# Feed-forward of an encoder layer: split weights carried over a half switch, own places for the first block, and a residual added by transfers

## The chip, the cores and the metric

The kernel runs on one core of one Trainium2 chip. The metric is device time in microseconds (us) of one execution, given as the median of three. The engines are TensorE (PE, matrix products), VectorE (DVE), ScalarE (ACT), GpSimd (POOL) and SyncE (SP). SP computes nothing here: it issues nearly all transfers, one after the other.

## The reference

One layer of a trunk over 2048 tokens of width 1024, in float32. `att_*` weights serve windowed attention, `ffn_*` the feed-forward; `mod` comes from a conditioning vector.

```python
h = rmsnorm(x, mix_norm_pre[i]) * (1.0 + sc1) + sh1
y = windowed_gqa_sink(h, att_w_qkv[j], att_w_o[j], att_sink[j], rel_bias)
x = x + g1 * rmsnorm(y, mix_norm_post[i])          # called x1 in the kernel
h = rmsnorm(x, ffn_norm_pre[i]) * (1.0 + sc2) + sh2
a, b = split(h @ ffn_w_in[i]); y = (silu(a) * b) @ ffn_w_out[i]   # 2816 hidden units
x = x + g2 * rmsnorm(y, ffn_norm_post[i])          # the output
```

## The kernel before, in words

Activations stand transposed, 128 features by 512 tokens to a tile; 512 tokens are a chunk, c = 0 to 3, and two chunks are a half, hf = 0 and 1. The row is: projections, attention with the output projection (`OProj`) of chunks 0 to 2 as filler, the output projection of chunk 3 alone (`last_o`), the hidden stage, the out stage. A scheduler that simulates the program fixes the order on every engine and every buffer's address; at run time each engine takes its instructions in that order and waits at semaphores.

Products keep float32's accuracy by splitting each operand into a rounded part hi and a rest lo, and adding three products (`three`, L149 to L151). A split is one cast on ACT (L154) and one subtraction on another engine, mostly DVE (L155).

The feed-forward uses Strassen's scheme in Winograd's form. A half's two chunks and pairs of feature tiles make 2x2 blocks, and seven products replace eight. The seven operands from activations are called b11, t2, b21, t3, t1, t4, b22 (`OPERANDS`, in the order of the steps); tile names are such as `hb11…` and `ht2…`. The sums among them lie in DRAM: `hd_d` and `h2_d` for the hidden stage, `g_d` for the out stage. The seven from weights (`wa11, ws2, wa12, ws3, ws1, wa22, ws4`) are made on the spot by a `Block`: two loads (`wiri` or `wiro`, L741, L742), four sums on DVE (L746 to L749), seven splits. In a block `step(i)` runs product i over m tiles; `take` folds the product from PSUM into the results.

*Hidden stage.* Blocks t = 0 to 21 (`Hidden`) for each half. A half's operands stay in memory for all its blocks. At the switch from half 0 to half 1 the blocks 20 and 21 go step by step in turn (`interleaved`), and after each step that operand of half 1 is loaded. `give_pair` writes results to `g_d`. Beside half 0 runs the generator `late`: it turns chunks 2 and 3 of the attention's result into half 1's operands, one piece per block. Each chunk needs two statistics (`rstd_of`), whose sum over features is a product with a matrix of ones, after a split of the sum by DVE (L129, L130), as `nstl` and `nstlo`.

*Start of it.* `last_o` uses memory on the right side that the feed-forward gets afterwards (`lasto.close()`). The second pool for split weights, `wr`, and the pool `hB` for t1, t4 and b22 are opened only then. So the first block's last three split weights and those operands wait for the end of `last_o`.

*Out stage.* The 11 hidden tile pairs are cut into parts, `PARTS = ((2, 3, 3, 3), (3, 3, 3, 2))` by half. For each part four blocks `Outs` (n2 = 0 to 3) run; a part's last two blocks are interleaved while the next part's operands load. Part 0 copies its products to results z on ACT (L947), the others add them to z on DVE (L950). Half 0's end (`ends`) runs beside half 1's first parts: the statistic of z, then `finish` per tile, which is z times r (L998), then times a coefficient and plus x1 (L999) on DVE, x1 having been loaded by SP.

*Last part.* It is computed plainly: product `pl` for chunk 2 over 512 columns, then chunk 3 in two halves of 256. After the last product come the sum of squares (`nstz`, L126), the statistic, `finish` for eight tiles (L998, L999) and the stores.

Of the kernel before, what the change touches and what calls it, by code (L numbers as in the profile page):

```python
# [11 lines left out]
F32 = mybir.dt.float32  # L12
# [45 lines left out]
PARTS = ((2, 3, 3, 3), (3, 3, 3, 2))  # L58
MD = max(max(p) for p in PARTS)

# [13 lines left out]
def encoder_layer(ctx, tc, a):  # L74
# [43 lines left out]
    def rstd_of(alloc, psp, ptag, acc, tag, r=None, direct=False):  # L118
# [122 lines left out]
    with ExitStack() as pa:  # L241
# [9 lines left out]
        sp.dma_start(gains, a["gains"])  # L251
        act.activation(cb, cb, AF.Silu)
# [278 lines left out]
    class OProj:  # L531
# [5 lines left out]
        def fill(self, prev=None, hold=None):  # L537
# [11 lines left out]
            for n in range(KT):  # L549
                w = wop.tile([P, 2, KT, P], F32R, tag="w", name=f"wo{c}_{n}", bufs=2)  # L550
                if c in (0, NCH - 1):
                    raw = wop.tile([P, KT, P], F32, tag="raw", name=f"wor{c}_{n}", bufs=3 if c else 2)
# [21 lines left out]
                else:  # L574
                    sq = yp.tile([P, CH], F32, tag="nsq", name=f"ysq{c}_{n}", bufs=4)
# [110 lines left out]

    lasto = ExitStack()
# [11 lines left out]
    ffn = ExitStack()  # L699
# [3 lines left out]
    wl, wr = open_pool(early, "wl"), None  # L703
# [9 lines left out]
    class Operands:  # L713
# [6 lines left out]
        def slot(self, n, k):  # L720
            t = (hA if n in OPERANDS[:nleft] else hB).tile([P, 2, CH], F32R, tag=n, name=f"h{n}{self.u}_{k}")
            self.ops[n][k] = (t[:, 0], t[:, 1])
            return self.ops[n][k]
# [9 lines left out]
    class Block:  # L733
# [39 lines left out]
    def give_pair(hf, j):  # L773
# [5 lines left out]
        if hf == S // HALF - 1 and j >= HT // 2 - PARTS[-1][-1]:  # L779
# [5 lines left out]
    class Hidden(Block):  # L785
        def __init__(self, half, t, hf):
            super().__init__(half, t, f"i{half.u}_{t}", a["w_in"][t], a["w_in"][HT + t])
            self.t, self.got, self.hf = t, {}, hf
# [39 lines left out]
    def interleaved(pair, nxt, end=iter(())):  # L828

        for i in range(7):  # L830
            for b in pair:
                b.step(i)
            next(end, None)
# [3 lines left out]
    def late_residuals():  # L837

        for c in range(CPH, NCH):
# [13 lines left out]
            rstd_of(temp, psF, "mm", acc, f"l{c}", r)  # L853
            yield
            for k in range(0, KT, 2):
# [33 lines left out]
    wr = open_pool(ffn, "wr", side="right")  # L889
# [5 lines left out]
    for hf in range(S // HALF):  # L895
        for t in range(HT - 2 if hf + 1 < S // HALF else HT - 1):
# [3 lines left out]
            next(late, None)  # L900
        if hf + 1 < S // HALF:
# [3 lines left out]
            interleaved(pair, half)  # L905
    assert next(late, None) is None
# [250 lines left out]
```

## Time and profile before

| | |
|---|---|
| median of 3 runs | 2168.6 us (2166.22 to 2171.56) |
| profiled execution | 2170.63 us, span 2168.8 us, mean granted TensorE clock 0.98 |
| instructions | 28917 |
| busy: PE, DVE, ACT, POOL | 94%, 76%, 50%, 34% of the span |
| moved | 396.35 MB, mean 183 GB/s |
| hidden stage to out stage | about 1700 us |

Busy time of PE contains matmuls that overlap; how many matmuls a stretch holds says more of its rate. Where PE waits, the view of waits names the engine and line that ended the wait.

### The profile page before, as it was taken

How to read it: one execution, taken by the hardware profiler on the slowest of the kernel's cores; microseconds unless marked ns; L12 is line 12 of the kernel's file. 1: busy time of each engine (PE TensorE's matmuls, PEld its weight loads, DVE VectorE, ACT ScalarE, POOL GpSimd, SP SyncE). 2: the span in 40 equal slices, each digit the busy share in tenths (PEclk: the TensorE clock that was granted, in tenths of full speed). 3: DMA queues.
4: the chain of work that ended last, by engine and by line, in shares of the span. 5: the costliest groups of instructions: out<-in, count | busy, mean ns of one | idle time of the engine just before them, and what ended most of it. 6: DMA issues, size and time to landing. Idle time of an engine off the chain costs nothing.

```text
span 2168.8 us, 28917 instructions
## 1 busy us (share of the span) xinstructions
PE 2044.4 (94%) x9366; PEld 1669.0 (77%) x9366; DVE 1646.5 (76%) x2933; ACT 1076.9 (50%) x2125; POOL 747.7 (34%) x687
## 2 busy tenths in 40 slices
PE   6898999989989888999999989999999899998997
PEld 4786877878767766878887868888888688867886
DVE  7656766665676658987878898766664788999997
ACT  4546666577787746343434352333332654465432
POOL 3404343366778711533354512322221200230040
PEclk8999999999999989999999999999999999999998
DMA  8887665576667694534454764323230544447542
GB/s 279 261 256 250 187 184 172 165 275 244 226 196 241 199 342 174 192 130 155 170 169 156 257 232 148 123 96 117 102 112 35 194 151 150 147 147 271 167 139 102
DMA packets 200516, 396.35 MB, mean 183 GB/s; under 512 B 20091, under 2 KB 62124, under 8 KB 195244
## 3 DMA queue, kind: packets, MB, share of 16 engines
q1 hardware_dynamic: 199788, 393.97, 54.5%
q8 instruction: 74, 1.21, 0.2%
q14 instruction: 78, 0.64, 0.1%
q10 hardware_dynamic: 576, 0.52, 0.1%
HBM read 270.65 MB, written 123.76 MB: 182 GB/s over the span
## 4 chain that ended last, share of the span: by engine, by line
PE 66%; DVE 15%; DMA 7%; issue 4%; ACT 3%; POOL 3%; SPq 1%; DVEq 0%; ACTq 0%; POOLq 0%
PE pc_i L149 10%; PE pc_i L150 10%; PE pc_i L151 10%; PE pc_o L151 4%; PE pc_o L149 4%; PE pc_o L150 4%; PE t L455 3%; PE s L432 3%; PE psq L149 2%; PE psq L151 2%; PE psq L150 2%; PE py L149 2%; PE py L151 2%; PE py L150 2%; PE o L461 2%
## 5 line engine op out<-in xcount | busy, mean ns | idle before, releaser
L437 DVE CUSTOM_DVE_ANT_0 pr<-s,bias,nsink 128x384 f32<-128x384 f32 (+1 forms) x256 | 149.2, 596 | 93.7 <-PE s L432 73.2
L149 PE MATMUL pc_i<-ht,ws_i 128*128 128x512 f32 x528 | 207.1, 392 | 9.3 <-ACT ws_i L154 5.2
L151 PE MATMUL pc_i<-ht,ws_i 128*128 128x512 f32 x528 | 206.5, 391 | 0.0
L150 PE MATMUL pc_i<-ht,ws_i 128*128 128x512 f32 x528 | 206.4, 391 | 0.0
L439 ACT ACTIVATE pr<-pr,nm 128x385 f32<-128x385 f32 (+1 forms) x256 | 153.8, 603 | 70.5 <-DVE nm L437 63.2
L823 POOL TENSOR_TENSOR p_i<-p_i,u_i 128x512 f32<-128x512 f32 x44 | 72.1, 1638 | 323.5 <-DVE u_i L810 166.1
L445 POOL TENSOR_SCALAR pr<-pr,rs 128x384 f32<-128x384 f32 (+1 forms) x256 | 147.5, 601 | 82.4 <-DVE rs L443 82.3
L954 POOL TENSOR_TENSOR z<-z,z 128x512 f32<-128x512 f32 x32 | 54.8, 1730 | 344.3 <-DVE z L950 314.4
L432 PE MATMUL s<-k,q 128*128 128x384 f32 (+1 forms) x512 | 136.1, 359 | 19.8 <-DVE nm L437 13.5
L149 PE MATMUL pc_i<-hb,wa_i 128*128 128x512 f32 x352 | 138.5, 394 | 0.3
L150 PE MATMUL pc_i<-hb,wa_i 128*128 128x512 f32 x352 | 138.2, 393 | 0.0
L151 PE MATMUL pc_i<-hb,wa_i 128*128 128x512 f32 x352 | 138.2, 392 | 0.0
L154 ACT CAST ws_i<-s_i 128x512 fp32r<-128x512 f32 x132 | 81.7, 619 | 113.5 <-PE pc_i L151 100.6
L155 DVE TENSOR_TENSOR plo<-t,phi 128x512 fp32r<-128x512 f32 x184 | 121.6, 684 | 16.7 <-ACT phi L154 15.3
L154 ACT CAST wa_i<-wiri 128x512 fp32r<-128x512 f32 x132 | 81.8, 619 | 95.9 <-PE pc_i L151 93.7
L149 PEld LDWEIGHTS pc_i<-ht,ws_i 128*128 128x128 f32 x528 | 99.9, 189 | 32.1 <-ACT ws_i L154 5.7
L432 PEld LDWEIGHTS s<-k,q 128*128 128x128 f32 x512 | 86.6, 193 | 44.7 <-DVE nm L437 27.8
L455 PE MATMUL t<-ident,pr 128*128 128x128 f32 x736 | 113.1, 273 | 3.6 <-POOL pr L445 2.7
L150 PEld LDWEIGHTS pc_i<-ht,ws_i 128*128 128x128 f32 x528 | 99.9, 189 | 20.8
L151 PEld LDWEIGHTS pc_i<-ht,ws_i 128*128 128x128 f32 x528 | 99.7, 189 | 20.9
L149 PE MATMUL py<-ol,wo 128*128 128x512 f32 x256 | 103.3, 405 | 11.8 <-ACT wo L154 7.9
L155 DVE TENSOR_TENSOR wa_i<-wiri,wa_i 128x512 fp32r<-128x512 f32 x132 | 107.6, 816 | 5.4 <-ACT wa_i L154 5.1
(320 smaller groups left out, 6131.5 us busy)
## 6 DMA issues: line engine op xcount, KB each, us to landing
wiri<-w_in SPq DMA_DIRECT2D x88, 512.0 KB, 4.7
ada<-ada_w SPq DMA_DIRECT2D x40, 512.0 KB, 5.0
wiro<-w_out SPq DMA_DIRECT2D x48, 384.0 KB, 3.8
q_d<-e SPq DMA_DIRECT2D x64, 256.0 KB, 4.0
q<-q_d SPq DMA_DIRECT2D x16, 1024.0 KB, 5.8
wo<-wo_d SPq DMA_DIRECT2D x16, 1024.0 KB, 5.9
g_d_b<-p_i SPq DMA_DIRECT2D x44, 256.0 KB, 4.8
g_d_t<-p_i SPq DMA_DIRECT2D x40, 256.0 KB, 2.0
```

The costliest lines, as they stand in the source:

```text
L149: pe.matmul(ps, w[0], h[0], start=first, stop=False)
L150: pe.matmul(ps, w[0], h[1], start=False, stop=False)
L151: pe.matmul(ps, w[1], h[0], start=False, stop=last)
L154: act.copy(hi, src)
L155: return eng.tensor_tensor(lo, src, f(hi), ALU.subtract).ins
L432: m = pe.matmul(ps[:, :n], q[:, h, jb * P:(jb + 1) * P], kk[:, i, (jb + j0) * P:(jb + j1) * P], start=i == 0, stop=i == 1)
L437: red = dve.tensor_tensor_reduce(pr[:, h, :n], ps[:, :n], bias[g][:, h, j0 * P:j1 * P], -1.0, nsink[:, hh:hh + 1], ALU.add, ALU.min, nm[:, ...
L439: act.activation(pr[:, h, :n + 1], pr[:, h, :n + 1], AF.Exp, bias=nm[:, h:h + 1], scale=-1.0, accum_out=rs[:, h:h + 1])
L445: pool.tensor_scalar(pr[:, h, :n], pr[:, h, :n], rs[:, h:h + 1], 1.0, ALU.mult, ALU.mult)
L455: pe.transpose(pt[:, h * P:(h + 1) * P], pr[:, h, jj * P:(jj + 1) * P], ident)
L823: pool.tensor_tensor(sa, sa, b, ALU.mult)
L954: (pool if (i, x) in ((2, 2), (4, 4), (5, 5), (6, 6)) else dve).tensor_tensor(sums[hf, n2, x], sums[hf, n2, x], sums[hf, n2, y], ALU.add)
```

## The change

In the feed-forward and around it:

- **Half switch.** Half 1 begins with blocks 20 and 21 and takes over the split weights that half 0 has just used (`like`): no loads, no sums, no splits. Its other blocks are 0 to 19, and 19 is the last. In the out stage half 0's last part and half 1's first part are now the same tiles, 8 to 10, and half 1 begins with the pair n2 = 2, 3 on the weights that half 0 ended with. The plainly computed last part becomes tiles 6 and 7.
- **Places.** `wr` and a pool `hR` for operand t1 are opened before `last_o`'s pools, which shrink (two raw buffers in place of three, two of `nsq` in place of four in chunk 3). In the out stage there are 6 and 8 buffers of split weights (before 5 and 6), and two temporaries in place of five.
- **Late work.** `LATE` says how many pieces of `late` run after each block of half 0: none after the first three. The statistics there use the float32 sum directly, without DVE's split.
- **Statistics.** `rstd_of` has two DVE instructions in its end in place of three; the gains are multiplied by -0.5 once at the start, on POOL.
- **Residual.** `finish` is one DVE instruction; x1 is then added by a transfer that POOL issues and that accumulates into the tile, and SP's store waits for it. In `ends` the tiles have four buffers.
- **Last part.** Four quarters of 256 columns (half of a chunk); `ENDS` spreads earlier quarters' `finish` over later ones. The last quarter keeps a product and a sum with loaded x1 on DVE. The order of DVE's instructions there is fixed by tokens.

```diff
-PARTS = ((2, 3, 3, 3), (3, 3, 3, 2))
+PARTS = (((0, 2), (2, 3), (5, 3), (8, 3)), ((8, 3), (0, 3), (3, 3), (6, 2)))
+LATE = 3 * (0,) + 2 * (1, 1, 2, 1, 1, 1) + (1, 1, 2, 1, 1)
...
-        dve.scalar_tensor_tensor(t, ps, EPS, t, ALU.add, ALU.mult)
-        dve.tensor_scalar(t, t, -0.5, 1.5, ALU.mult, ALU.add)
-        dve.tensor_tensor(r, r, t, ALU.mult)
+        order(dve.scalar_tensor_tensor(t, ps, EPS, t, ALU.add, ALU.mult))
+        order(dve.scalar_tensor_tensor(r, t, -3.0, r, ALU.add, ALU.mult))
...
+    ffn = ExitStack()
+    wr = open_pool(ffn, "wr", side="right")
+    hR = open_pool(ffn, "hR", KT // 2, side="right")
     lasto = ExitStack()
...
-        def __init__(self, ops, i, u, wa, wb):
+        def __init__(self, ops, i, u, wa, wb, like=None):
             self.ops, self.u, m = ops, u, ops.m
+            if like is not None:
+                self.w = like.w
+                return
...
             sp.dma_start(acc, acc_d[c - CPH])
-            rstd_of(temp, psF, "mm", acc, f"lo{c}", r)
             yield
+            rstd_of(temp, psF, "mm", acc, f"lo{c}", r, direct=True)
...
     lasto.close()
-    wr = open_pool(ffn, "wr", side="right")
     hB = open_pool(ffn, "hB", K2, side="right")
...
-        for t in range(HT - 2 if hf + 1 < S // HALF else HT - 1):
+        for t in range(HT - 2 - hf):
...
-            next(late, None)
+            for _ in range(1 if hf else LATE[t]):
+                next(late, None)
...
             interleaved(pair, half)
+            interleaved([Hidden(half, b.t, hf + 1, b) for b in pair], None)
...
-    def finish(c, k, r, xr, cols=slice(0, CH), engs=(dve, dve)):
-        y, xr = ys[c, k][:, cols], xr[:, cols]
-        engs[0].tensor_tensor(y, y, r, ALU.mult)
-        engs[1].scalar_tensor_tensor(xr, y, coef[:, 3, k:k + 1], xr, ALU.mult, ALU.add)
-        (act if k % 2 and cols.stop - cols.start < CH and cols.start else sp).dma_start(out[c, :, k, cols], xr)
+    def finish(c, k, r, z, cols=slice(0, CH), order=lambda m: m):
+        z = z[:, cols]
+        order(dve.scalar_tensor_tensor(z, ys[c, k][:, cols], coef[:, 3, k:k + 1], r, ALU.mult, ALU.mult))
+        pool.dma_start(z, x1_d[c][:, k, cols], accum_op=ALU.add)
+        sp.dma_start(out[c, :, k, cols], z)
...
-            for n2 in range(KT // 2 - 2):
+            n2s = list(range(KT // 2))
+            if hf and p == 0:
+                n2s = n2s[2:] + n2s[:2]
+                like = [Outs(ops, hf, p, b.n2, b) for b in pair]
+                interleaved(like, None, end, 2)
...
+    parts = [(c, slice(i * CH // 2, (i + 1) * CH // 2)) for c in range(NCH - CPH, NCH) for i in range(2)]
...
+            if i and n == 3:
+                tail_rstd(i - 1)
+            for _ in range(ENDS[i][n] if n < KT else 0):
+                tail_finish(*ending.pop(0))
```

Line numbers shift by 4 to 40 in the new file; `three` is L153 to L155 there, a split L158 and L159.

**Order, first place: SP at the end of chunk 2's output projection.** `wo2_7` is that projection's last weight tile; `hd_d…` are stores of half 0's operands, `hf…` loads for them, `ol3…` the attention result that `last_o` multiplies. Before:

```order
L543 DMA ol3_0_8380<-o_d3_0_120 128x1024
L558 DMA wo2_7_8307<-wo_d7_351 128x2048
L469 DMA o_d3_3_123<-of15_3_8060 256x1x128
L611 DMA hd_d0_0_t3_305<-y1_0_6053 128x512
L579 DMA y_d0_340<-y2_5_8232 128x512
L502 DMA h2_d1_337<-y1_4_6625 128x512
L611 DMA hd_d0_0_t2_304<-y1_1_6244 128x512
```

Now:

```order
L616 DMA hd_d0_1_t1_310<-hf2_8237 128x512
L616 DMA hd_d0_0_t2_304<-y1_1_6240 128x512
L616 DMA hd_d0_0_t4_307<-hf1_8187 128x512
L614 DMA hf3_8238<-h2_d0_336 128x512
L507 DMA h2_d1_337<-y1_4_6620 128x512
L507 DMA h2_d1_337<-y1_5_6735 128x512
L563 DMA wo2_7_8300<-wo_d7_351 128x2048
```

The load of `wo2_7` stands behind a store of `t4` (from `hf1`, DVE's last sum of that group) and a load that it stood ahead of. The first `ol3` load, ahead of `wo2_7` before, comes here now:

```order
L616 DMA hd_d0_2_t4_315<-hf5_8289 128x512
L614 DMA hf6_8339<-h2_d0_336 128x512
L548 DMA ol3_0_8379<-o_d3_0_120 128x1024
L584 DMA y_d0_340<-y2_7_8327 128x512
L614 DMA hf7_8340<-h2_d0_336 128x512
L548 DMA ol3_1_8383<-o_d3_1_121 128x1024
L548 DMA ol3_2_8387<-o_d3_2_122 128x1024
```

Its wait there is for the last matmul of `py2_7`, whose memory it takes; the loads of `wor3_0` and `wor3_1` (`last_o`'s raw weights) have moved ahead of all these rows.

**Second place: ACT at the start of the hidden stage.** Casts of operands t4 (`ht40…`) and b22 (`hb220…`) and of split weights of block 0, 1 and 2 (`ws1_i0_0` is block 0's). Before:

```order
L154 CAST ht40_2_8796<-ht40_2_8796 128x512
L154 CAST ht40_3_8800<-ht40_3_8800 128x512
L154 CAST hb220_0_8804<-hb220_0_8804 128x512
L154 CAST hb220_1_8808<-hb220_1_8808 128x512
L819 ACT_TABLE_LOAD
L819 ACTIVATE p1_i0_0_8867<-p1_i0_0_8867 128x512
L154 CAST hb220_2_8812<-hb220_2_8812 128x512
L154 CAST hb220_3_8816<-hb220_3_8816 128x512
L154 CAST ws1_i0_0_8845<-s1_i0_0_8826 128x512
L154 CAST wa22_i0_0_8848<-wiri0_0_8823 128x512
L154 CAST ws4_i0_0_8851<-s4_i0_0_8828 128x512
L154 CAST wa11_i0_1_8988<-wiri0_1_8978 128x512
```

Now:

```order
L158 CAST wa11_i0_2_9116<-wiri0_2_9106 128x512
L158 CAST ws2_i0_2_9119<-s2_i0_2_9110 128x512
L158 CAST wa12_i0_2_9122<-wiri0_2_9106 128x512
L158 CAST ws3_i0_2_9125<-wiri0_2_9106 128x512
L158 CAST ht40_0_8784<-ht40_0_8784 128x512
L158 CAST ht40_1_8788<-ht40_1_8788 128x512
L158 CAST ws4_i0_1_8985<-s4_i0_1_8962 128x512
L158 CAST ws1_i0_2_9128<-s1_i0_2_9109 128x512
L158 CAST ht40_2_8792<-ht40_2_8792 128x512
L158 CAST ht40_3_8796<-ht40_3_8796 128x512
L158 CAST hb220_0_8800<-hb220_0_8800 128x512
L158 CAST hb220_1_8804<-hb220_1_8804 128x512
```

Block 0's weights are no longer in this stretch (they are split earlier); t4 and b22 have moved behind block 1's and much of block 2's weights. PE's order there, `pc5_i0_0` and `pc6_i0_0` being block 0's sixth and seventh product:

```order
L155 MATMUL pc4_i0_0_8910<-ht10_3_8780,ws1_i0_0_8841 128x512
L153 MATMUL pc5_i0_0_8926<-ht40_0_8784,wa22_i0_0_8844 128x512
L153 MATMUL pc6_i0_0_8941<-hb220_0_8800,ws4_i0_0_8847 128x512
L153 MATMUL pc0_i0_1_8988<-hb110_0_8695,wa11_i0_1_8967 128x512
L154 MATMUL pc0_i0_1_8988<-hb110_0_8695,wa11_i0_1_8967 128x512
```

PE takes one matmul each on the first t4 and b22 tile, and then goes on with block 1.

**Third place: DVE at the end of half 0's out stage**, where `z…` are half 0's results, `nrz0` their statistic and `zx…` what is stored. Before:

```order
L139 SCALAR_TENSOR_TENSOR ntz0_0_17899<-nstz0_0_17897,ntz0_0_17899 128x512
L155 TENSOR_TENSOR ws3_o1_0_3_18185<-wiro1_0_3_18166,ws3_o1_0_3_18185 128x384
L140 TENSOR_SCALAR ntz0_0_17899<-ntz0_0_17899 128x512
L141 TENSOR_TENSOR nrz0_0_17896<-nrz0_0_17896,ntz0_0_17899 128x512
L998 TENSOR_TENSOR z0_0_2_15779<-z0_0_2_15779,nrz0_0_17896 128x512
L998 TENSOR_TENSOR z0_0_5_15806<-z0_0_5_15806,nrz0_0_17896 128x512
L998 TENSOR_TENSOR z0_1_2_15873<-z0_1_2_15873,nrz0_0_17896 128x512
L998 TENSOR_TENSOR z0_1_5_15900<-z0_1_5_15900,nrz0_0_17896 128x512
```

Now:

```order
L144 SCALAR_TENSOR_TENSOR ntz0_0_17791<-nstz0_0_17789,ntz0_0_17791 128x512
L756 TENSOR_TENSOR s1_o1_0_1_18000<-wiro1_0_1_17997 128x384
L145 SCALAR_TENSOR_TENSOR nrz0_0_17788<-ntz0_0_17791,nrz0_0_17788 128x512
L757 TENSOR_TENSOR s2_o1_0_1_18001<-s1_o1_0_1_18000,wiro1_0_1_17997 128x384
L758 TENSOR_TENSOR wiro1_0_1_17997<-wiro1_0_1_17997 128x3x128
L159 TENSOR_TENSOR wa22_o1_0_0_17991<-wiro1_0_0_17966,wa22_o1_0_0_17991 128x384
L1003 SCALAR_TENSOR_TENSOR zx0_0_17797<-z0_0_2_15690,coef_361,nrz0_0_17788 128x512
L1003 SCALAR_TENSOR_TENSOR zx0_1_17801<-z0_0_5_15717,coef_361,nrz0_0_17788 128x512
L1003 SCALAR_TENSOR_TENSOR zx0_2_17829<-z0_1_2_15784,coef_361,nrz0_0_17788 128x512
L1003 SCALAR_TENSOR_TENSOR zx0_3_17833<-z0_1_5_15811,coef_361,nrz0_0_17788 128x512
```

The three instructions of a statistic are two, the product L998 is gone, and the finished tile is written by one instruction (L1003).

More of the change, by code (lines that the diff above doesn't have):

```diff
@@ L832, in interleaved @@
                 b.step(i)
-            next(end, None)
+            for _ in range(ends):
+                next(end, None)
             if nxt is not None:
@@ L1104, in _bucket @@
+    assert not ending
+    tail_rstd(3)
+    r = rs_[c][:, cols]
+    for n in range(KT + 1):
+        if n < KT:
+            y = ys[c, n][:, cols]
+            tail(dve.tensor_tensor(y, y, r, ALU.mult))
+        if n:
+            k, x = n - 1, late_x[n - 1]
+            tail(dve.scalar_tensor_tensor(x, ys[c, k][:, cols], coef[:, 3, k:k + 1], x, ALU.mult, ALU.add))
+            (act if k % 2 else sp).dma_start(out[c, :, k, cols], x)
 def _bucket(n):
```

127 lines of the change are left out of this document (66 added, 61 removed).

## The prediction

> **What bounds the kernel now.** I read the page's busy times and chain first, then stretches, then PE's waits, then the timeline where a wait is large.
>
> ```profile
> PE 2044.4 (94%) x9366; PEld 1669.0 (77%) x9366; DVE 1646.5 (76%) x2933; ACT 1076.9 (50%) x2125; POOL 747.7 (34%) x687
> PE 66%; DVE 15%; DMA 7%; issue 4%; ACT 3%; POOL 3%; SPq 1%; DVEq 0%; ACTq 0%; POOLq 0%
> ```
>
> PE is busy almost throughout, and the change takes no product away: it can only win back PE's pauses. The table of stretches shows where these are. The columns give PE's busy time, and in brackets how many matmuls began.
>
> ```profile
> core 0: us, PE busy (x) PEld busy (x) DVE busy (x) ACT busy (x) POOL busy (x), PEclk, DMA share, GB/s
> 740.00:780.00 40.00, 28.43 (x101) 21.36 (x100) 22.80 (x27) 19.31 (x26) 17.74 (x12) 0.83 0.94 341
> 820.00:860.00 40.00, 34.77 (x143) 28.16 (x142) 32.80 (x51) 22.78 (x37) 6.97 (x4) 0.91 0.54 191
> 900.00:960.00 60.00, 55.11 (x230) 44.71 (x229) 48.48 (x63) 22.32 (x38) 27.34 (x19) 0.94 0.47 156
> 1120.00:1160.00 40.00, 37.67 (x159) 30.72 (x158) 30.75 (x44) 17.41 (x28) 14.05 (x11) 0.96 0.44 145
> 1240.00:1320.00 80.00, 73.16 (x313) 57.79 (x312) 78.93 (x122) 35.37 (x65) 18.77 (x13) 1.00 0.66 227
> 1400.00:1480.00 80.00, 80.00 (x354) 66.24 (x353) 58.56 (x87) 25.73 (x43) 18.54 (x12) 1.00 0.30 105
> 1680.00:1720.00 40.00, 33.15 (x132) 25.56 (x131) 27.80 (x57) 23.62 (x50) 14.66 (x2) 0.94 0.57 204
> 1900.00:2000.00 100.00, 89.32 (x372) 69.60 (x371) 99.86 (x170) 61.94 (x122) 16.30 (x8) 0.97 0.60 207
> ```
>
> The row 1400 to 1480 has no pause: 354 in 80 us, 0.226 us each. Against that pace the others lack 76, 34, 35, 18, 41, 45 and 70 matmuls: 17, 8, 8, 4, 9, 10 and 16 us, 72 in all, slow clock after pauses included. Here are PE's waits from 740 us on, in us, with their number and the longest:
>
> ```profile
> PE pc_o L149 <- DVE z L950: 8.1, 3, 6.8
> PE py L149 <- ACT wo L154: 7.9, 1, 7.9
> PE nstl L131 <- DVE nhil L129: 6.0, 2, 3.7
> PE pc_i L149 <- ACT ws_i L154: 5.2, 1, 5.2
> PE py L149 <- DMA wo<-wo_d: 3.6, 2, 3.1
> PE pc_i L149 <- ACT p_i L794: 3.3, 2, 2.1
> ```
>
> **The change part by part.** The order before 740 us is shuffled by the shorter statistics; nothing there is aimed at, and I count 0, within 4 either way (a DVE instruction of 512 columns less per statistic, 0.68 us by the L528 row below).
>
> *End of chunk 2's projection.* Times of before, by queue and engine:
>
> ```profile
> 750.11 0.32 SPq L558 DMA_DIRECT2D wo<-wo_d  x1
> 756.09 0.68 DVE L528 TENSOR_TENSOR hf<-hf,y 128x512 f32<-128x512 f32 x1
> 763.34 1.71 SPq L543 DMA_DIRECT2D ol<-o_d  x2
> 765.61 0.69 ACT L570 ACTIVATE y<-py,coef 128x512 f32<-128x512 f32 x1 [7.89 <-PE py L151]
> 769.83 1.04 ACT L154 CAST ol<-ol 128x1024 fp32r<-128x1024 f32 x1 [3.04 <-DMA ol<-o_d]
> ```
>
> The load of `wo2_7` went out at 750.1 and PE waited 3.1 for it, to about 757.8. Now it stands behind the store of DVE's L528 (done at 756.8 before). DVE reaches that sum later: two splits of `last_o`'s weights stand ahead of it, and the statistic it hangs on ends later in PE's row. I put it at 757 to 758; four issues of about 0.4 follow, so the load goes out near 759.5, 9 us later, and PE's 3.1 grow to about 12. If DVE's splits don't wait, the load goes out as early as before, and nothing is lost; if they wait 2 us more, PE waits 14. Then `last_o`'s operand: its load could go out 2 us before the projection ended; now it must wait for that end. From issue (763.3) to the end of the first cast (770.9) took 7.5, so PE stands about 7.5 there again, instead of 7.9. The raw weights, which come earlier, no longer matter. Sum: +8 (range 0 to +11).
>
> *Start of the hidden stage.* The wait of 5.2 was for block 0's `ws1`:
>
> ```profile
> 821.58 0.69 ACT L570 ACTIVATE y<-py,coef 128x512 f32<-128x512 f32 x1 [3.10 <-PE py L151]
> 836.09 0.61 ACT L154 CAST ws_i<-s_i 128x512 fp32r<-128x512 f32 x1
> 836.61 0.61 ACT L154 CAST wa_i<-wiri 128x512 fp32r<-128x512 f32 x1
> ```
>
> It goes. But t4 and b22 are now cast behind nine casts of blocks 1 and 2, which themselves wait for the silu after block 0's third product. From the end E of `last_o` (821.5) PE has 32 matmuls, 7.2 us, before its first t4 matmul, and right behind it the first b22 matmul. ACT reaches the silu at E+3, block 1's sums on DVE hold its casts to about E+7.5, four of block 2 and then six (0.52 each by the last two rows) bring the first b22 cast to E+13. PE would wait about 5.5 in place of 5.2, with the same slow clock. I take -1 (range -7 to +2): the stall changes its name.
>
> *Late work.* The two waits for L129 (6.0) fall away with the split; a float32 sum costs PE about 0.45 us more than two rounded ones (the sums at the end, below: 3.6 us for eight of 256 columns, so 0.9 for 512, against 0.45), four times. The two waits for L794 (3.3) come when temporaries run short; the delay of three blocks meets them. I take -7 of the 12 that the stretches 900 and 1120 lack and these 3.3 (range -3 to -11).
>
> *Half switch.* DVE is busy 78.9 of 80 us, and it is what PE waits for. By form, in that stretch:
>
> ```profile
> L155 DVE TENSOR_TENSOR wa_i<-wiri,wa_i 128x512 fp32r<-128x512 f32 x12 | 11.3, 944 | 0.0
> L746 DVE TENSOR_TENSOR s_i<-wiri 128x512 f32<-128x512 f32 x4 | 3.8, 954 | 0.0
> ```
>
> Two blocks without four sums and seven splits each are 22 instructions of 0.68 to 0.95, 15 to 21 us off DVE, on the very stretch. Of the 9 us lacking I take -8 (range -4 to -9). The carried weights hold their buffers one pair longer; the next block's splits have that pair's 38 us (168 matmuls) to follow.
>
> *Hidden to out stage.* One POOL product took 13 us beside a row of DVE instructions, and SP's store of it held the loads behind it:
>
> ```profile
> 1698.66 13.34 POOL L823 TENSOR_TENSOR u_i<-u_i,b_i 128x512 f32<-128x512 f32 x1 [3.69 <-ACT u_i L819]
> 1712.03 0.33 SPq L778 DMA_DIRECT2D g_d_b<-u_i  x1
> ```
>
> The last block is now a pair whose sums go through DVE, so DVE itself waits for that product, and part 0's operand loads stand ahead of the store. Of 10 us I take -5 (range 0 to -8).
>
> *Out stage, 1900 to 2000.* DVE is busy 99.9 of 100 us; PE lacks 16.
>
> ```profile
> L998 DVE TENSOR_TENSOR z<-z,nrz 128x512 f32<-128x512 f32 x16 | 9.8, 681 | 0.1
> L155 DVE TENSOR_TENSOR ws_o<-s_o,ws_o 128x384 fp32r<-128x384 f32 x18 | 9.8, 544 | 0.0
> ```
>
> ```profile
> g_d_b<-p_i SPq DMA_DIRECT2D x44, 256.0 KB, 4.8
> ```
>
> L998's 16 products go (10 us), and two blocks' weights (22 instructions of about 0.55, 12 us): 22 us less on a saturated engine. I take -11 (range 0 to -15), since `finish` may now stop DVE: the fifth tile waits for the first one's accumulation and store. Neither an accumulating transfer nor one issued by POOL is in the trace; from the write (0.7) and two transfers like the page's `g_d_b<-p_i`, the nearest by size (4.8 each), a round takes about 10 us, against 13 DVE instructions of about 0.6 between. POOL's own combining (L954) then queues behind 16 issues, and frees z later; part 0 needs it only two pairs on.
>
> *End.*
>
> ```profile
> 2148.13 0.28 PE L150 MATMUL pl<-gls,wl 128*128 128x256 f32 x1
> 2148.25 0.28 PE L151 MATMUL pl<-gls,wl 128*128 128x256 f32 x1
> 2149.53 3.62 PE L126 MATMUL nstz<-zsl,ones 128*128 128x256 f32 x16
> 2155.96 0.47 ACT L136 ACTIVATE nrz<-nstz,epsc 128x256 f32<-128x256 f32 x1 [4.14 <-DVE z L998]
> 2155.78 3.25 DVE L999 SCALAR_TENSOR_TENSOR zx<-z,coef,zx 128x256 f32<-128x256 f32 x8
> 2160.18 2.77 DVE L998 TENSOR_TENSOR z<-z,nrz 128x256 f32<-128x256 f32 x8
> 2162.87 3.25 DVE L999 SCALAR_TENSOR_TENSOR zx<-z,coef,zx 128x256 f32<-128x256 f32 x8
> ```
>
> From the last product to the span's end pass 20.5 us. The sum of squares ends at 2153.2, but its logarithm starts at 2156.0 and DVE's part at 2159, behind the previous half's L999. With earlier quarters finished earlier: 4.9 to the end of the sums, 1.3 on ACT, 0.9 on DVE, 6.0 for L998 and L999, 2.7 from DVE's end to the span's: 15.8, so -4.7. Chunk 2 in halves costs 192 matmuls of 0.12 (the first two rows) for 96 of 0.226, +1.3. Sum -3.5 (range -6 to +4, if the 24 accumulations outlast the last quarter).
>
> Sum: 8 - 1 - 7 - 8 - 5 - 11 - 3.5 = -27.5. The profiled execution took 2170.6, 2.0 above the median; from the median the forecast is 2141.
>
> A rule speaks against the main doubt. By the Trainium skill, page "SBUF — State Buffer", section "Who interferes with whom", a DVE instruction with two inputs in SBUF holds up a GpSimd instruction that reads SBUF, not one that only writes. The POOL row of 13.34 us agrees with its first half; if the second holds, POOL's issues would not be starved, and the -11 stands; if they were, the rival below gives the time. No run of before shows an issue by POOL.
>
> **The rivals.**
>
> *The stalls only move.* The first two parts already do. If DVE stays saturated in the out stage because freed time is taken up by splits that the scheduler put earlier, -11 becomes -4, the half switch -4, hidden to out 0: about -12, 2157. For it: PE follows a fixed order. Against: 22 us off DVE.
>
> *Accumulation holds DVE* (slower). If each of POOL's issues is starved like the product of 13.3 us, a round of four tiles takes 13.3 and twice 4.8 and 0.7, 23.6 us; four rounds are 94 us beside a stretch whose products take 57 (252 matmuls). DVE stands at the fifth tile, PE behind DVE: +37 in place of -11, total about +20, 2189. It decides from a round of about 21 us. Against: DVE, once it waits, no longer starves POOL.
>
> *More than forecast.* The projection's end costs nothing (DVE gets there in time), and the ranges' better ends hold: about -50, 2119.
>
> *No change.* Gains of about 8 only, with the +8 of the first part and a longer end: 2167.
>
> **How the numbers follow.** Forecast 0.65, stalls move 0.16, more 0.09, accumulation 0.06, no change 0.04. The forecast's own range is 2125 to 2153. The range 2118 to 2160 takes in "more" and "stalls move", and leaves out the last two and some of the edges. A measurement of this kernel tells about 0.3%, 6.5 us, from no change: faster 0.87, same 0.06, slower 0.07.
>
> **What would show it.** Right: PE's wait for `wo<-wo_d` near 12 us; a wait for a cast of `hb` or `ht` in place of `ws_i` near 829; no `nhil` among the waits; 1240 to 1320 near 350 matmuls; 1900 to 2000 shifted, with over 415; under 17 us from the last `pl` to the end. Wrong: DVE waiting for stores at L1003, SP's loads late behind `out<-zx`, or a POOL product of over 10 us in the out stage.

## The result, and the profile after

The changed kernel takes 2191.6 us (median of 4 runs, 2187.8 to 2193.1) against 2170.1 us for the kernel before (4 runs, 2166.2 to 2173.6): ratio 1.0097, 95% interval 1.0074 to 1.012. It is slower by 1%, where 2141 was forecast. The profiled execution took 2193.05 us, its span 2191.1 us.

DVE lost the work that the change takes from it (1646.5 us before), and PE has 98 matmuls more, 96 of them from the chunk in halves:

```profile
PE 2055.1 (94%) x9464; PEld 1681.5 (77%) x9464; DVE 1594.1 (73%) x2857; ACT 1063.7 (49%) x2108; POOL 781.2 (36%) x728
```

So 52 us less on DVE bought nothing. The stretches after, with the columns as before (busy time and, in brackets, matmuls that began; full pace is 178 in 40 us, 531 in 120):

```profile
760.00:800.00 40.00, 18.17 (x58) 13.44 (x57) 24.33 (x22) 14.27 (x20) 13.52 (x8) 0.71 0.90 320
960.00:1000.00 40.00, 31.84 (x135) 25.89 (x134) 30.86 (x39) 15.01 (x25) 19.82 (x15) 0.91 0.59 191
1200.00:1240.00 40.00, 36.61 (x149) 29.38 (x148) 31.36 (x42) 17.48 (x26) 17.27 (x12) 0.91 0.61 207
1240.00:1360.00 120.00, 116.14 (x504) 93.77 (x503) 102.44 (x156) 44.63 (x78) 40.59 (x26) 1.00 0.65 226
1920.00:2040.00 120.00, 108.75 (x445) 85.61 (x444) 98.66 (x164) 61.18 (x120) 28.12 (x24) 0.96 0.63 178
```

The first row is the deepest hole: 58 matmuls, where before the poorest 40 us there had 101. PE's waits from 740 us on name its cause:

```profile
PE py L153 <- DMA wo<-wo_d: 14.5, 1, 14.5
PE pc_i L153 <- ACT p_i L804: 11.6, 2, 8.2
PE py L153 <- ACT ol L158: 7.2, 1, 7.2
PE pc_i L153 <- ACT ht L158: 3.0, 1, 3.0
PE pc_i L153 <- ACT hb L158: 2.6, 1, 2.6
PE py L153 <- ACT ysq L581: 2.1, 1, 2.1
```

Next I took the last matmul of each stage from the timeline, first of before, then of after: attention (`o`), output projection (`py`), hidden stage (`pc_i`), out stage (`pc_o`) and last part (`pl`, of before 2148.25).

```profile
747.21 0.39 PE L461 MATMUL o<-plo,v 128*128 128x512 f32 x1
821.15 0.40 PE L151 MATMUL py<-ol,wo 128*128 128x512 f32 x1
1692.87 0.40 PE L151 MATMUL pc_i<-hb,ws_i 128*128 128x512 f32 x1
2102.43 0.40 PE L151 MATMUL pc_o<-hb22o,ws_o 128*128 128x512 f32 x1
```

```profile
751.09 0.40 PE L466 MATMUL o<-plo,v 128*128 128x512 f32 x1
849.49 0.40 PE L155 MATMUL py<-ol,wo 128*128 128x512 f32 x1
1716.04 0.40 PE L155 MATMUL pc_i<-hb,ws_i 128*128 128x512 f32 x1
2125.79 0.40 PE L155 MATMUL pc_o<-hb22o,ws_o 128*128 128x512 f32 x1
2173.05 0.28 PE L155 MATMUL pl<-gls,wl 128*128 128x256 f32 x1
```

| stretch | before | after | difference | forecast |
|---|---|---|---|---|
| to attention's end | 747.2 | 751.1 | +3.9, with moved products +8.2 | 0 |
| output projection | 73.9 | 98.4 | +24.5, without moved products +14.7 | +8 |
| hidden stage | 871.7 | 866.6 | -5.2, with moved products 0 | start -1, late work -7, half switch -8 |
| out stage | 409.6 | 409.8 | +0.2 | hidden to out -5, out -11 |
| last part to its last `pl` | 45.8 | 47.3 | +1.4 | +1.3 |
| tail | 20.6 | 18.1 | -2.5 | -4.7 |

The moved products change the bookkeeping only. 24 matmuls of the first block (28 in place of 4) now stand ahead of the last `py`: at 0.226 us each 5.4 us. And 19 of chunk 2's projection now stand behind attention's last matmul (PE began 3425 matmuls up to there before, 3406 after): 4.3 us. The rows sum to 22.3 us, the difference of the spans.

The first row comes from one execution of each kernel and is not firm: all the kernels below that begin the same 3406 matmuls up to attention's end reach it between 744.8 and 752.0 us. The other rows repeat better; the projection takes 97.7 to 99.7 us in the seven kernels that have its long wait.

### The profile page after: what moved, and what is told of

Read it like the earlier page. It is cut to its first block, busy times and chain, and to the rows that moved or that the text cites. A ratio compares the mean times of both kernels' runs of the same rounds, so it can differ in the third digit from the quotient of the medians.

```text
span 2191.1 us, 29147 instructions
## 1 busy us (share of the span) xinstructions
PE 2055.1 (94%) x9464; PEld 1681.5 (77%) x9464; DVE 1594.1 (73%) x2857; ACT 1063.7 (49%) x2108; POOL 781.2 (36%) x728
## 5 line engine op out<-in xcount | busy, mean ns | idle before, releaser
L153 PE MATMUL pc_i<-ht,ws_i 128*128 128x512 f32 x528 | 206.0, 390 | 2.7 <-DVE p_i L809 0.8
L155 PE MATMUL pc_i<-ht,ws_i 128*128 128x512 f32 x528 | 205.7, 390 | 0.0
L159 DVE TENSOR_TENSOR plo<-t,phi 128x512 fp32r<-128x512 f32 x184 | 121.6, 685 | 26.2 <-ACT phi L158 24.9
L153 PE MATMUL pc_i<-hb,wa_i 128*128 128x512 f32 x352 | 139.9, 397 | 0.0
L155 PE MATMUL pc_i<-hb,wa_i 128*128 128x512 f32 x352 | 137.8, 391 | 0.0
L158 ACT CAST ws_i<-s_i 128x512 fp32r<-128x512 f32 x126 | 77.7, 618 | 121.5 <-PE pc_i L155 118.2
L158 ACT CAST wa_i<-wiri 128x512 fp32r<-128x512 f32 x126 | 78.1, 620 | 107.5 <-PE pc_i L155 107.2
L153 PE MATMUL py<-ol,wo 128*128 128x512 f32 x256 | 102.9, 406 | 25.3 <-DMA wo<-wo_d 14.5
L460 PE MATMUL t<-ident,pr 128*128 128x128 f32 x736 | 117.5, 279 | 4.4 <-POOL pr L450 3.6
L153 PEld LDWEIGHTS pc_i<-ht,ws_i 128*128 128x128 f32 x528 | 99.2, 188 | 24.9 <-issue 1.9
L154 PEld LDWEIGHTS pc_i<-ht,ws_i 128*128 128x128 f32 x528 | 99.3, 188 | 20.6
L155 PEld LDWEIGHTS pc_i<-ht,ws_i 128*128 128x128 f32 x528 | 99.1, 188 | 20.6
L158 ACT CAST phi<-t 128x512 fp32r<-128x512 f32 x184 | 101.5, 588 | 26.5 <-PE t L460 21.4
```

The lines of the kernel that those rows point to most:

```text
L153: pe.matmul(ps, w[0], h[0], start=first, stop=False)
L154: pe.matmul(ps, w[0], h[1], start=False, stop=False)
L155: pe.matmul(ps, w[1], h[0], start=False, stop=last)
L158: act.copy(hi, src)
L159: return eng.tensor_tensor(lo, src, f(hi), ALU.subtract).ins
L460: pe.transpose(pt[:, h * P:(h + 1) * P], pr[:, h, jj * P:(jj + 1) * P], ident)
```

## The experiments

Labels as c1 are those of the runs: c1 has places undone, c2 the load issued by ACT, c3 late even, c4, f3 and g1 the three on the kernel before, h1 the statistics of before, d1 and d2 the two pairs, d3 and f2 the carried weights, d4 and f4 the residual, f1 and h2 all three causes out. Each kernel below is the changed one with the edit shown, unless the text says "on the kernel before". The ratio is always to the kernel before, run on the same chip. "Late even" is one piece of late work after every block; "places" are the pools that the change opens ahead of `last_o`'s.

### Whose is the wait at the projection's end?

**Places undone.**

```diff
...
-    wr = open_pool(ffn, "wr", side="right")
-    hR = open_pool(ffn, "hR", KT // 2, side="right")
     lasto = ExitStack()
...
     lasto.close()
-    hB = open_pool(ffn, "hB", K2, side="right")
+    wr = open_pool(ffn, "wr", side="right")
+    hB = hR = open_pool(ffn, "hB", K2, side="right")
```

> The changed kernel with the places undone: the second pool of split weights and t1's operand are opened after the last output projection again, with its buffers as before (three raw, four of squares). Theory (the moved places set the order at the end of chunk 2's projection): the load of its last weight tile stands ahead of the t4 store again, PE's wait of 14.5 us for it falls under 4, the first operand of the last projection is loaded before that projection ends, and the total falls by 12 to 18 us, to 2174 to 2180; the wait for a cast of ht and hb at the start of the hidden stage (5.6) is replaced by one for ws_i of about 5. Rival (the shorter statistic alone sets that order): the 14.5 stays and the total moves by under 5.

Measured: 2168.1 us, ratio 0.9977 (0.9966 to 0.9987). The wait for `wo2_7` was 7.8, not under 4; the last `py` came at 824.65, and the total fell by more than the 12 to 18 us expected. One part of the change, undone, gives back all of the loss.

**Load of `wo2_7` issued by ACT**, past SP's queue.

```diff
-                    sp.dma_start(f(w), wo_d[n])
+                    (act if c == NCH - 2 and n == KT - 1 else sp).dma_start(f(w), wo_d[n])
```

> The changed kernel, but the load of chunk 2's last projection weight is issued by ACT and not by SP, so that it is behind nothing of SP's queue. Theory (the 14.5 us are SP standing before DVE's sums): the wait falls to 0 to 4 us, the total by 9 to 14, to 2178 to 2183; the wait for the last projection's first operand stays at about 7, since its load still has to wait for that projection's last matmul. Rival (the transfer itself is slow there, or DMA is full): the wait stays over 10.

Measured: 2177.3 us, ratio 1.0017 (1.0005 to 1.0029); wait 5.1, a little above the 0 to 4 expected. So the queue ahead of that load is the greater part of the wait, but the way round it doesn't reach what c1 does.

**On the kernel before: places alone, statistics alone, both.** The edits are the change's own.

```diff
-        dve.tensor_scalar(t, t, -0.5, 1.5, ALU.mult, ALU.add)
-        dve.tensor_tensor(r, r, t, ALU.mult)
+        dve.scalar_tensor_tensor(r, t, -3.0, r, ALU.add, ALU.mult)
...
```

> The kernel before with the places alone. Its order puts the last weight's load ahead of the t4 store, but the last projection's first operand behind it. Theory (both parts, places and shorter statistics, are needed for the 14.5): PE waits under 5 for the weight tile, about 7 to 8 for the operand, and at the start of the hidden stage about 5 for casts of ht and hb in place of ws_i: total within 5 us of before, 2165 to 2175. Rival (the places alone cost it): 10 to 20 us slower than before.

> The kernel before with the shorter statistics alone (two DVE instructions, gains scaled once). Its order moves the load of chunk 2's last projection weight behind ten more rows of SP, though not behind the t4 store. Theory (part of the 14.5 us comes from this part): PE's wait for that tile grows from 3 to 6 to 9 us, and the total by 2 to 8, to 2174 to 2181. Rival (the shorter statistics gain in attention what they lose there): within 2 us of before.

> The kernel before with both the places and the shorter statistics, nothing else. In its order the last weight's load stands behind the t4 store, as in the changed kernel and in neither of the two alone. Theory (the 14.5 us come from these two parts together): PE waits 12 to 15 us for that tile and 6 to 8 for the operand, and the total is 10 to 20 us above the 2166 of the shorter statistics alone. Rival (a third part, as the late work, is needed): the wait stays under 9.

Measured: places alone 2172.7 us, ratio 1.0006 (0.9992 to 1.002); statistics alone 2165.8, 0.9962 (0.9947 to 0.9977), where 2174 to 2181 was expected; both 2180.8, 1.0047 (1.0031 to 1.0063). PE's waits, one row of each in that order:

```profile
PE py L149 <- DMA wo<-wo_d: 3.4, 1, 3.4
```

```profile
PE py L148 <- DMA wo<-wo_d: 7.8, 1, 7.8
```

```profile
PE py L148 <- DMA wo<-wo_d: 15.3, 1, 15.3
```

Neither part makes the long wait (the statistics alone make half of it); together they do, and two parts that are neutral and faster alone come out slower. The mechanism is in the timeline. Statistic `nx` of chunk 2 (its second matmul on PE) and POOL's eight products with it, of before and then of after:

```profile
736.10 0.39 PE L132 MATMUL nstx<-nlox,ones 128*128 128x512 f32 x1
741.28 11.39 POOL L500 TENSOR_TENSOR y<-y,nx 128x512 f32<-128x512 f32 x8 [7.14 <-DVE nx L141]
```

```profile
749.46 0.39 PE L137 MATMUL nstx<-nlox,ones 128*128 128x512 f32 x1
755.54 13.76 POOL L505 TENSOR_TENSOR y<-y,nx 128x512 f32<-128x512 f32 x8 [0.63 <-DVE nx L145]
766.42 1.76 DVE L531 TENSOR_TENSOR y<-y,hf 128x512 f32<-128x512 f32 x1
768.21 1.64 DVE L533 TENSOR_TENSOR hf<-hf,y 128x512 f32<-128x512 f32 x1
769.87 0.32 SPq L616 DMA_DIRECT2D hd_d_t<-hf  x1
771.73 0.43 SPq L563 DMA_DIRECT2D wo<-wo_d  x1
```

With the shorter statistic that matmul stands 1.6 us ahead of attention's last one (751.09) where it stood 11.1 ahead (747.21), 13 us later in all; f3 and g1, which have the shorter statistic too, show the same place. POOL's products, DVE's sums and the t4 store follow 12 to 14 us later. The load of `wo2_7` goes behind that store only where both parts meet: issued at 771.7, not 759.5. With the statistics alone it goes out ahead of the sum (f3: 760.9, the sum at 770.5), and so it does with the places and the old statistics (h1 below: 751.9, the sum at 757.8). The same sums take 1.6 to 1.8 us here, beside POOL's products, against 0.68 before (the L528 row at 756.09, while POOL was idle).

**Statistics of before, rest as changed**, the test of that reading.

```diff
-        pool.tensor_scalar(gains, gains, -0.5, 1.0, ALU.mult, ALU.mult)
...
-        order(dve.scalar_tensor_tensor(r, t, -3.0, r, ALU.add, ALU.mult))
+        order(dve.tensor_scalar(t, t, -0.5, 1.5, ALU.mult, ALU.add))
+        order(dve.tensor_tensor(r, r, t, ALU.mult))
```

> The changed kernel with the statistics of before (three DVE instructions, gains not scaled); all else as changed. Theory: the two-instruction statistic moved chunk 2's statistic nx about 13 us later in every engine's order (its second matmul 736.1 before, 749.5 after), with it POOL's eight products and DVE's sums, and the places put the load of wo2_7 behind the last of these. With the old statistic nx comes early again: its last instruction about 6 us ahead of the end of attention instead of 3 us behind it, POOL's products of L505 before about 755, PE's wait for wo<-wo_d 3 to 5 us in place of 14.5, a wait for ol of 8 to 10, last py 12 to 16 us earlier against the end of attention, time 2175 to 2180. Rival: the places alone make the wait (smaller buffers for wor and nsq): the wait stays at 12 to 15 and the time at 2188 to 2193.

```profile
PE pc_i L154 <- ACT p_i L804: 13.3, 1, 13.3
PE py L154 <- ACT ol L159: 10.1, 1, 10.1
PE py L154 <- DMA wo<-wo_d: 4.0, 2, 3.5
```

```profile
742.96 11.40 POOL L505 TENSOR_TENSOR y<-y,nx 128x512 f32<-128x512 f32 x8 [7.16 <-DVE nx L146]
```

The mechanism came out as expected: POOL's products at 743, the wait 4.0, the load issued at 751.9, and the last `py` 83.6 us behind attention's end against 98.4. The time followed only in part: 2186.2 us (2182.3 to 2189.2), ratio 1.0066 (1.0048 to 1.0085), above the 2175 to 2180 expected. In the profiled execution, the fastest of the four, the projection's 14.8 us are there, but the hidden stage was 3.7 us longer and the out stage 2.3. The late work's stall at 980 us grew (first row) and a later one went: from 900 to 1240 us PE began 1416 matmuls, against 1422.

### Late work

**Late even.**

```diff
-LATE = 3 * (0,) + 2 * (1, 1, 2, 1, 1, 1) + (1, 1, 2, 1, 1)
+LATE = 20 * (1,)
```

> The changed kernel with one piece of the late work after each block of half 0 (as before the change), the statistics still on the float32 sum. Theory (thicker late work makes ACT's copies wait): PE's waits for the cast or copy of p_i, 11.6 us in two places, fall to under 5, the total by 6 to 12, to 2180 to 2186. Rival (they come from other changes, as the order of loads): they stay, within 3 us.

Measured: 2180.2 us, ratio 1.0036 (1.0024 to 1.0047). The hidden stage took 859.5 us in place of 866.6, and the stretch 960 to 1000 has no pause left:

```profile
960.00:1000.00 40.00, 40.00 (x177) 32.73 (x175) 30.75 (x44) 16.45 (x27) 12.55 (x8) 1.00 0.35 119
```

The stall that it removes, on ACT and DVE of the changed kernel:

```profile
990.07 0.69 DVE L513 TENSOR_TENSOR ly<-ly,lx 128x512 f32<-128x512 f32 x1 [2.63 <-POOL ly L512]
990.85 0.63 ACT L519 ACTIVATE xsq<-ly 128x512 f32<-128x512 f32 x1 [4.34 <-issue]
991.38 0.57 ACT L804 COPY p_i<-pc_i 128x512 f32<-128x512 f32 x1
```

ACT's copy of a product, for which PE waits 8.2 us, stands in ACT's order behind a square of the late work, which waits for a chain SP, POOL (L512), DVE (L513). My reading is that two pieces after one block bring more such squares than the chain can feed in that time; that even pieces remove the stall is shown. They also undo the delay of three blocks; with 20 pieces for 20 blocks no run has the delay without the density.

**Places undone and late even; the same with the load by ACT.**

> The changed kernel with places undone and the late work even, both at once. Theory (the two losses are independent): what the two runs alone won adds up, 23 and 11 us, so 2155 to 2161, faster than the kernel before by 11 to 17 us. Rival (once one wait is gone the other grows): no better than 2165.

> The same, and the load of chunk 2's last projection weight issued by ACT. With places undone PE still waited 7.8 us for that tile; by ACT it should wait 2 to 5: total 3 to 6 us under the kernel with both undone. Rival (the wait is the transfer beside the other loads): no difference over 2 us.

Measured: 2162.4 us, ratio 0.9947 (0.993 to 0.9963), and 2164.3, 0.9957 (0.9943 to 0.997). The two causes nearly add: 29 us where the two alone gave 23 and 11, just above the 2155 to 2161 expected. The load by ACT cut the wait from 7.8 to 4.4 and the projection by 1.9 us (72.5 to 70.5), but the total shows no gain.

### The carried weights

**Half 1's first pair splits its weights again**, in the hidden stage (d3), in the out stage (f2).

```diff
-            interleaved([Hidden(half, b.t, hf + 1, b) for b in pair], None)
+            interleaved([Hidden(half, b.t, hf + 1) for b in pair], None)
```

```diff
-                like = [Outs(ops, hf, p, b.n2, b) for b in pair]
+                like = [Outs(ops, hf, p, b.n2) for b in pair]
```

> The changed kernel, but half 1's first two hidden blocks load, sum and split their weights again, in the same order of blocks. Theory (DVE's saved work is what shortens the half switch): PE lacks 6 to 12 us more between 1240 and 1400 than in the changed kernel (27 matmuls, 6 us there), total +4 to +10. Rival (the order of blocks, in turn by pairs, gives the time, not the saved work): within 2 us.

> The changed kernel, but half 1's first pair of out blocks loads, sums and splits its weights again. Theory (the saved 12 us of DVE are of use): PE lacks 3 to 12 us more between 1920 and 2040, total 2194 to 2204. Rival (DVE isn't the limit there any more; SP's order is): within 3 us of the changed kernel.

Measured: 2191.2 us, ratio 1.0077 (1.0061 to 1.0094), and 2196.9, 1.0106 (1.0084 to 1.0129). Neither can be told from the changed kernel by its time. The stretches say a little more: 1240 to 1360 of d3, then 1920 to 2040 of f2.

```profile
1240.00:1360.00 120.00, 114.63 (x496) 91.97 (x495) 110.84 (x169) 49.48 (x88) 37.51 (x25) 1.00 0.66 232
```

```profile
1920.00:2040.00 120.00, 103.54 (x414) 80.39 (x414) 102.98 (x174) 62.54 (x127) 30.35 (x24) 0.93 0.64 189
```

Without the carry 8 matmuls fewer at the half switch (2 us) and 31 fewer in the out stage (7 us). The stages agree: d3's hidden stage is 2.7 us longer than that of the changed kernel, f2's out stage 7.1.

### The residual by transfers

**Half 0's finish on DVE** with x1 loaded by SP, as before.

```diff
-                finish(c, k, r, z)
+                sp.dma_start(z, x1_d[c][:, k, :])
+                dve.tensor_tensor(ys[c, k], ys[c, k], r, ALU.mult)
+                dve.scalar_tensor_tensor(z, ys[c, k], coef[:, 3, k:k + 1], z, ALU.mult, ALU.add)
+                sp.dma_start(out[c, :, k, :], z)
```

> The changed kernel, but in half 0's end x1 is loaded by SP and product and sum stand on DVE as before; the tail is left. Theory A (the accumulating transfers hold SP's queue, 33 us of waits, and so the next part's operands): PE lacks less between 1920 and 2040 than the 19 us of the changed kernel, by 5 or more. Theory B (DVE's saved 11 us outweigh that): it lacks 5 to 11 us more. Neither: within 3, the transfers trade one wait for another.

**Half 0's stores issued by POOL**, the accumulation kept.

```diff
-        sp.dma_start(out[c, :, k, cols], z)
+        (sp if c >= NCH - CPH else pool).dma_start(out[c, :, k, cols], z)
```

> The changed kernel, but in half 0's end POOL issues the store behind each accumulating transfer, so that SP's queue waits for none of them. Theory (SP standing before those stores is what delays the next part's operands): the out stage wins most of the 10 us that finishing on DVE won, total 2180 to 2186. Rival (DVE's wait for one of four buffers is what costs): DVE waits the same or more, no gain, 2189 or more.

Measured: 2181.1 us, ratio 1.0032 (1.0018 to 1.0046), and 2186.3, 1.0053 (1.0039 to 1.0068), the second just above its 2180 to 2186. The stretch 1920 to 2040 of the two (x445 in the changed kernel):

```profile
1920.00:2040.00 120.00, 115.24 (x491) 93.43 (x491) 113.04 (x190) 66.09 (x128) 13.94 (x8) 0.97 0.58 193
```

```profile
1920.00:2040.00 120.00, 112.88 (x469) 90.03 (x468) 101.94 (x171) 63.71 (x126) 37.31 (x40) 0.96 0.63 184
```

With 14 us more work on DVE the stretch holds 46 matmuls more, and the out stage takes 399.6 us in place of 409.8. In the changed kernel two in-order rows wait there, DVE's and then SP's:

```profile
DVE zx L1003 <- DMA out<-zx: 11.5, 7, 2.3
```

```profile
SPq L1005 <- DMA zx<-x_d: 32.7, 15, 6.2
```

SP's stores wait 32.7 us for POOL's accumulations, and what stands behind them on SP is the loads of the next operands. DVE's seven waits are for one of four buffers. Moving the stores off SP gave 24 of the 46 matmuls back, with DVE's waits unchanged (11.0): about half of the cost is SP's queue (by the length of the out stage 3.9 of the 10.2 us). In that run the stores wait in POOL's queue instead, 24.0 us, so the other half is not shown to be DVE's waits.

### All three causes out

**Places undone, late even, half 0's finish on DVE; and the same with the places kept and the statistics of before.** No new edit.

> The changed kernel with places undone, late work even, and half 0's end finished on DVE with loaded x1: all three losses found so far taken away, the carried weights, the direct statistics and the tail kept. Theory (they add): 11 us below the 2162 of the kernel with the first two undone, if nothing else fills the gap: 2149 to 2157, faster than before by 15 to 22 us. Rival: in that kernel the out stage had already lost less, so the gain there is under 4, 2158 or more.

> The changed kernel with the statistics of before, one piece of late work after each block, and half 0's finish as product and sum on DVE with x1 loaded by SP; places and carried weights stay. Theory: the three causes add (about 13, 11 and 10 us of 2191.6): 2155 to 2160, and no better than with the places undone (2154), since the operand wait of 8 to 10 us at the end of the projection stays in place of a wait of 4 us for block 0's weights. Rival: with the wait for wo2_7 gone, the places pay after all (last_o begins earlier and block 0's weights are ready): 2143 to 2150.

Measured: 2154.1 us, ratio 0.9909 (0.9894 to 0.9925), and 2158.3, 0.9935 (0.991 to 0.9961). Both beat both kernels. What is left of the change in the first (mainly carried weights, shorter statistics, the last part in quarters) makes the kernel 0.9% faster. No run shows that the places pay: without the long wait h2, which has them, is not faster than f1, which has not (the intervals overlap, and the statistics differ too), and on the kernel before they were neutral (c4). At the projection's end and behind it PE waits 9.7 us for `ol`, 4.0 for `wo<-wo_d` and 2.6 for `hb` in h2, and 7.9 for `wo2_7` and 4.4 for `ws_i` in f1.

## Why the prediction was wrong

Forecast -27.5, measured +22 in the profiled runs. By the rows of the table, moved products put back, the projection cost 14.7 us in place of 8, the hidden stage gained nothing in place of 16, the out stage with its start nothing in place of 16, and attention's end came 8.2 later in place of 0, which is not firm. Most of the miss is thus gains that did not come. Two steps failed above all: that a delay of the late work frees PE, where its denser rest stalls ACT; and that the accumulation costs DVE a wait and SP nothing. Three further gains were too large, and one cost was too small.

*End of chunk 2's projection, +8 forecast, +14.7 measured: wrong in size.* The queue position was right (the load stands behind the t4 store), and so was the operand wait (7.5 forecast, 7.2 measured). The failing step is "I put it at 757 to 758" for DVE's last sum; it came at 768.2. The prediction saw that the statistic ends later in PE's row, but gave it a microsecond or two where it took 13, since the shuffle before 740 us was counted at 0. That this late statistic makes the wait is shown by h1, where it is early and the wait 4.0, and that it needs the places beside it by f3 and g1. The wait itself, 14.5 where about 12 was forecast, came near by luck: the load went out 12 us later than forecast, but PE too reached it 10 us later (765.1 in place of 755.1). The two long waits are 10.7 of the 14.7 us (14.5 and 7.2 against 3.1 and 7.9); waits of 2.1 for `ysq` and 1.6 for `last_o`'s weights, which the sum left out, make most of the rest.

The slow clock is not part of it. It cost the kernel before as much, here behind the second long wait of before and then of after:

```profile
773.50 0.79 PE L149 MATMUL py<-ol,wo 128*128 128x512 f32 x1 [7.93 <-ACT wo L154]
780.29 0.39 PE L149 MATMUL py<-ol,wo 128*128 128x512 f32 x1
```

```profile
794.38 1.22 PE L153 MATMUL py<-ol,wo 128*128 128x512 f32 x2 [7.24 <-ACT ol L158]
800.68 0.39 PE L154 MATMUL py<-ol,wo 128*128 128x512 f32 x1
```

From the first row to the second PE began 15 and 14 matmuls, most of them 0.43 us apart in place of 0.23. Behind the first long wait, 3.1 and 14.5 us, it was nine in both kernels, for 3.6 and 3.9 us.

Alone on the kernel before, places and statistics together cost 0.5%, 10 us (g1), near the +7 of the first two terms; in the changed kernel the places cost 1.2% (c1).

*Start of the hidden stage, -1: right.* The wait for `ws_i` (5.2) turned into waits for `ht` and `hb` (3.0 and 2.6), forecast 5.5.

*Late work, -7 forecast, about +4: wrong in sign.* The waits for `nhi` are gone, as said. But the two stretches now lack 42 and 28 matmuls, 16 us, where before they lacked 12 us. The step that failed is that "the delay of three blocks meets" the waits for the copy `p_i` (L794, now L804): they grew from 3.3 to 11.6. I counted what the delay frees and not what the denser schedule that follows it queues on ACT. c3 shows it: 7 us of the hidden stage.

*Half switch, -8 forecast, about -3.* In a window of 120 us around it, 504 matmuls after against 490 before:

```profile
1220.00:1340.00 120.00, 113.16 (x490) 90.89 (x489) 111.80 (x170) 46.96 (x85) 33.44 (x22) 1.00 0.61 211
```

DVE was no longer saturated (102 of 120 us), yet 27 matmuls are still lacking. "It is what PE waits for" took a busy engine for the bound of the whole deficit; d3, which gives DVE its work back, loses only 2 us. Its rival, that the order of the blocks gives the gain, fits, but was not tried by itself.

*Hidden to out, -5 forecast, about -3.* Over 140 us the stretch holds 582 matmuls after (1663 to 1803) and 568 before (1640 to 1780).

*Out stage, -11 forecast, about +3: wrong in sign.* 120 us from 1920 on hold 445 matmuls, where before 120 us from 1900 on held 460. That DVE waits at the fifth tile did occur, with the round near the 10 us forecast (first write 1962.9, fifth 1972.9). The failing step is its price: it was charged to DVE alone and not to SP, whose stores wait for each accumulation with the next loads behind them. The prediction named "SP's loads late behind `out<-zx`" as a sign of being wrong and put them at nothing. PE's waits of 3.3 us for `hb22o` and 2.3 for `ht1o` and `ht4o` in that stretch are absent in d4. The carried weights did bring their part (7 us, f2); the accumulation took it back (10 us, d4). Another 4 us stand in every variant of the changed kernel, d4 and f1 too, and not in the kernel before: PE waits for the sum of squares of half 0's statistic. No run takes them out, and their cause is open.

```profile
PE nstz L131 <- DVE zacc L994: 4.0, 1, 4.0
```

The slower rival's reason did not hold: POOL's issues were not starved, and the round took 10 us, not 21. That its 2189 lies near the measured 2191.6 is luck.

```profile
1962.93 2.73 DVE L1003 SCALAR_TENSOR_TENSOR zx<-z,coef,nrz 128x512 f32<-128x512 f32 x4
1972.91 0.75 DVE L1003 SCALAR_TENSOR_TENSOR zx<-z,coef,nrz 128x512 f32<-128x512 f32 x1 [2.31 <-DMA out<-zx]
1989.52 0.88 POOL L1004 DMA_DIRECT2D zx<-x_d  x1 [8.11 <-DVE zx L1003]
```

The 16 issues took 0.86 to 1.50 us, 0.88 in the median: 0.89 at 1969.8, beside DVE sums with two inputs, and 0.88 at 1974.0, with DVE nearly idle. By the Trainium skill, page "SBUF — State Buffer", section "Who interferes with whom", a DVE instruction with two inputs in SBUF contends with a GpSimd instruction that reads SBUF and not with one that only writes. The trace agrees on the first half, and on the second if an issue only writes: 0.88 us with and without DVE here, and above, DVE's sums at 1.76 in place of 0.68 beside POOL's products (1.72 each in place of 1.42).

*End.* The last `pl` came 1.4 later (1.3 forecast). The tail shrank by 2.5, not 4.7:

```profile
2173.16 3.61 PE L131 MATMUL nstz<-zs,ones 128*128 128x256 f32 x16
2184.21 0.87 DVE L1140 SCALAR_TENSOR_TENSOR zx<-z,coef,zx 128x256 f32<-128x256 f32 x2
2186.38 0.33 SPq L1005 DMA_DIRECT2D out<-z  x1
2186.81 1.36 SPq L1141 DMA_DIRECT2D out<-zx  x3
```

DVE ended 12.0 us behind the last `pl` (13.1 forecast). But its last stores went out at 2186.8, behind stores on SP that wait for accumulations (`out<-z`), and the span ended 6 us after DVE in place of 2.7.

Of the effects that the runs separate, the places on top of the shorter statistics cost 1.2% (c1), the late work 0.6% (c3, of which its hidden stage shows 7 us, 0.3%) and the accumulation 0.65% (d4); together taken out they give 1.9% (f1), less than the sum of 2.5%, though the intervals don't exclude it. Why h1's hidden and out stages were 6 us longer is not settled: its spread of 7 us over four runs is as large as the question. That the sums' 1.6 to 1.8 us come from POOL being beside them is read from the rows and wasn't tried alone. One side sum of the prediction is off and decided nothing: the better ends of its ranges, with the projection at 0, add up to -56 and not to about -50.

## What to carry to other kernels

A shortened instruction sequence can reorder everything around it, so compare the orders of every engine that feeds a moved transfer, not only the queue in which it stands. An engine freed of work gains nothing where the substitute puts waits into an in-order queue that also carries the next loads: price an accumulating transfer by what stands behind its store. And test the parts of a change in pairs too, since two parts that were neutral and faster alone were slower together.

## What the runs showed of the hardware

An accumulating transfer of 128x512 issued by POOL cost POOL 0.88 us in the median, and the first round (write, accumulate, store, buffer free) took 10 us. A DVE sum with two inputs took 1.6 to 1.8 us beside POOL's products and 0.68 with POOL idle. After pauses of PE of 3.1, 14.5, 7.9 and 7.2 us matmuls began 0.43 us apart in place of 0.23, for 3.6, 3.9, 6.8 and 6.3 us: the slow stretch did not grow with the pause.
